# Sliding-window attention inside a stream of projections: one TensorE visit per query tile that holds scores of tile n, transposes of tile n-1 and outputs of tile n-2

## The chip, the cores and the metric

The kernel runs on one core of one Trainium2 chip. The metric is the device time of one execution in microseconds (us), smaller is better; a time given for a kernel is the median of its runs. The engines of the core are called PE (TensorE, matrix products; its weight loads are listed as PEld), DVE (VectorE), ACT (ScalarE), POOL (GpSimd) and SP (SyncE, which here only issues transfers). Each has its own queue of instructions, written in program order.

## What is computed

One inference step of a two-layer decoder trunk with width 2048: 272 prompt rows (16 meta tokens and 256 tokens) and 64 sample rows (8 sequences of 8 tokens). Layer 0 is a gated linear recurrence, layer 1 is sliding-window attention with sinks, 32 query heads of 64 that share 4 key heads, window 128. The change is in layer 1, whose core in the reference is

```python
def sink_attention(q, k, v, mask, sinks):
    s = jnp.einsum('bnqhgd,bnshd->bnhgqs', q, k) * SWA_SCALE
    s = jnp.where(mask[None, :, None, None], s, -jnp.inf)
    sink = sinks.astype(jnp.float32)[None, None, :, :, None, None]
    m = jnp.maximum(jnp.max(s, axis=-1, keepdims=True), sink)
    p = jnp.exp(s - m)
    p = p / (jnp.sum(p, axis=-1, keepdims=True) + jnp.exp(sink - m))
    return jnp.einsum('bnhgqs,bnshd->bnqhgd', p, v)
```

It is used for the prompt (keys of the 144 or 256 positions that a block of queries can see) and for the samples (128 cached keys of each sequence and its own 8 new ones). The result is multiplied with SiLU of a gate projection and goes through the output projection. Everything is float32 to the reader; the large projections are done as three products of float32r halves (weights and inputs are each split into a high and a low part).

## The kernel before

**The stream of projections.** All large products run through one `Stream` (lines 111 to 224). A tile is 128 output columns of a weight; it takes 16 rounds (`kk`), each with three matmuls (L213, L214, L215) on one 128x128 piece of weight, and after each round `step()` is called. A *step* in this document is one such round. `run` also issues, ahead of use, the weight transfers on SP (`raw`, L147, four buffers), the high parts on ACT (`conv_hi`, L158) and the low parts on DVE (`conv`, L169).

**Everything else hangs on steps.** A piece of other work is a Python generator given to `spawn`. `step` (L173) goes through the list in order of spawning and resumes those that are due, at most two per step; `yield k` makes a generator due again k steps later, `yield 0` at the next step. What a generator issues between two yields stands together in the queues of the engines. The order on every engine is thus fixed when the program is written: if PE's next instruction has to wait, the projections behind it wait too.

**Layer 1.** The stream runs the key tiles k0, k1, value tiles v0, v1, then 16 query tiles `q1_j` and 16 gate tiles `g1_j`, then the output projection. When a tile is done, its epilogue spawns a chain. `unfold` (L870) applies the layer norm of layer 0 to the projection: a copy on ACT (L874), two DVE instructions (L876, L878), and an ACT instruction (L880), ten steps in all. Query tile j holds two query heads; four successive tiles share one key head q = j // 4.

**Prompt attention, `prompt_chain(j)` (L1012).** After `unfold`, the query is split (ACT and DVE, L265, L266) and three steps later twelve score matmuls are issued (L1030: keys in 64 rows of the array, the two heads beside each other). One step later DVE scales and masks (L1036), finds maxima (L1039), and `softmax` (L994) goes on: 4 steps later exponentials on ACT (L1003), 3 steps later sums and normalisation on DVE (L1006 to L1009), then 5 steps of pause. Then eight transposes by PE (L1046 to L1050), a step later their copies (ACT L1054, L1055; DVE L1056), 4 steps later the outputs: `vm1` (L1061) and `vm2` (L1064) with 128 key rows, `vm0` (L1067) with 16 key rows, each for the two heads into 64 columns of the array. A step later ACT copies them into `oT` (L1071). Each product that isn't float32r leaves two records.

**Sample attention, `sample_chain(q, u)` (L1073).** It is spawned behind the query tiles j with j % 4 of 1 and 2, so eight times, and handles four sequences: loads of cached keys (`cd`, twice, L1079) and values (`cv`, L1081) on SP, 12 steps later four transposes of keys (L1085) and a copy to `kzs` (L1087), after the fourth query tile of the head 32 small score matmuls (L1097), softmax, four transposes (L1112, L1113), copies (L1116, L1117), and outputs: two products with the 64 new value rows (L1121) and eight with cached values (L1126), copied to `oT` by four DVE instructions (L1131). So the PE part of the attention is made of separate visits between the projections, three for each query tile and four for each sample part.

**PSUM.** The projections use the pool `pj` (three banks), scores `lv` (two), transposes and outputs `mm` (three).

**The end of the attention.** `counted` (L979) keeps the number of unfinished chains in `L["att"]`; the chain of a gate tile (`epi_gg`, L1135) waits with `yield 0` until it is 0, then frees the attention's memory and multiplies gate and output.

## Time and profile before

| | us |
|---|---|
| median of 3 runs | 1181.28 |
| lowest and highest run | 1179.55, 1181.58 |
| the profiled execution | 1182.2 |
| its span, first to last instruction | 1180.4 |

The profile is of one execution. Its page gives busy time for each engine, then the chain of work that ended last, followed back from the last instruction, and groups of instructions by line. Matmuls are pipelined: a matmul is listed with its start and a modelled length of about 0.3 us, while the next can start 0.15 us later, so what one costs is read from the starts. The share of each engine hides that stages differ; by slices of a fortieth of the span (29.5 us), DVE's busy share in tenths and PE's are:

```profile
PE   8999999999999999999999999999999999999995
...
DVE  4766565656565666565668777577878867777674
ACT  4654554544554544554544445566656655554431
```

The attention is issued from about 754 to 952 us, that is, slices 26 to 33.

### The profile page before, as it was taken

What the parts mean: (1) busy time and instruction counts of PE and PEld (TensorE: products, weight loads), DVE (VectorE), ACT (ScalarE), POOL (GpSimd) and SP (SyncE); (2) the same over time, 40 slices, a digit from 0 to 9 for tenths busy, and PEclk for the clock granted to TensorE, in tenths of its full rate; (3) what the DMA queues carried; (4) which work ended last, traced back from release to release, by engine and by line L of the source; (5) the groups of instructions that cost most, each with busy time, mean ns of one, the idle gap of its engine ahead of it and who ended that gap; (6) DMA issues with size and microseconds to landing.
All of it is one profiled execution on the core that took longest, in us unless ns stands there. A gap on an engine that the chain in (4) does not pass through costs nothing.

```text
span 1180.4 us, 26871 instructions
## 1 busy us (share of the span) xinstructions
PE 1159.5 (98%) x10421; PEld 1117.4 (95%) x10421; DVE 789.0 (67%) x2080; ACT 602.8 (51%) x1777; POOL 236.5 (20%) x348
## 2 busy tenths in 40 slices
PE   8999999999999999999999999999999999999995
PEld 8999999999999999999999999988888899999994
DVE  4766565656565666565668777577878867777674
ACT  4654554544554544554544445566656655554431
POOL 3031221211211212211223331000000011154311
PEclk9999999999999999999999999999999999999998
DMA  9654565445555445555455545634244345556532
GB/s 263 181 146 129 162 175 151 136 139 146 162 166 161 131 132 159 161 164 156 119 145 150 142 142 169 184 103 121 87 116 118 93 139 147 150 152 187 140 99 90
DMA packets 328928, 171.51 MB, mean 145 GB/s; under 512 B 19164, under 2 KB 325692, under 8 KB 328758
## 3 DMA queue, kind: packets, MB, share of 16 engines
q1 hardware_dynamic: 327296, 167.77, 50.5%
q8 instruction: 82, 1.34, 0.5%
q10 hardware_dynamic: 960, 1.05, 0.3%
q0 software_dynamic: 544, 0.97, 0.3%
q14 instruction: 46, 0.38, 0.1%
HBM read 156.97 MB, written 14.42 MB: 145 GB/s over the span
## 4 chain that ended last, share of the span: by engine, by line
PE 94%; DMA 2%; POOL 1%; DVE 1%; ACT 1%; issue 0%; SPq 0%; POOLq 0%; DVEq 0%; ACTq 0%
PE pj_q L213 7%; PE pj_g L213 7%; PE pj_g L214 7%; PE pj_g L215 7%; PE pj_q L214 6%; PE pj_q L215 6%; PE pj_f L213 3%; PE pj_i L213 3%; PE pj_i L215 3%; PE pj_i L214 3%; PE pj_f L214 3%; PE pj_f L215 3%; PE pj_z L215 3%; PE pj_z L214 3%; PE pj_z L213 3%; PE pj_y L215 3%
## 5 line engine op out<-in xcount | busy, mean ns | idle before, releaser
L213 PE MATMUL pj_q<-xh,wlo_q 128*128 128x336 f32 (+1 forms) x512 | 167.5, 327 | 0.0
L213 PE MATMUL pj_g<-xh,wlo_g 128*128 128x336 f32 (+1 forms) x512 | 163.4, 319 | 0.0
L214 PE MATMUL pj_q<-xl,whi_q 128*128 128x336 f32 (+1 forms) x512 | 161.0, 314 | 0.0
L215 PE MATMUL pj_q<-xh,whi_q 128*128 128x336 f32 (+1 forms) x512 | 160.8, 314 | 0.0
L214 PE MATMUL pj_g<-xl,whi_g 128*128 128x336 f32 (+1 forms) x512 | 160.7, 314 | 0.0
L215 PE MATMUL pj_g<-xh,whi_g 128*128 128x336 f32 (+1 forms) x512 | 160.4, 313 | 0.0
L213 PEld LDWEIGHTS pj_q<-xh,wlo_q 128*128 128x128 f32 x512 | 96.8, 189 | 5.1 <-issue 2.2
L213 PEld LDWEIGHTS pj_g<-xh,wlo_g 128*128 128x128 f32 x512 | 96.6, 189 | 1.0 <-issue 0.5
L214 PEld LDWEIGHTS pj_q<-xl,whi_q 128*128 128x128 f32 x512 | 97.1, 190 | 0.0
L215 PEld LDWEIGHTS pj_q<-xh,whi_q 128*128 128x128 f32 x512 | 97.0, 190 | 0.0
L214 PEld LDWEIGHTS pj_g<-xl,whi_g 128*128 128x128 f32 x512 | 96.8, 189 | 0.0
L215 PEld LDWEIGHTS pj_g<-xh,whi_g 128*128 128x128 f32 x512 | 96.6, 189 | 0.0
L169 DVE TENSOR_TENSOR wlo_g<-raw_g,whi_g 128x512 fp32r<-128x512 f32 x128 | 90.8, 744 | 0.7 <-ACT whi_g L158 0.6
L169 DVE TENSOR_TENSOR wlo_q<-raw_q,whi_q 128x512 fp32r<-128x512 f32 x128 | 85.0, 684 | 5.4 <-ACT whi_q L158 5.4
L213 PE MATMUL pj_f<-xh,wlo_f 128*128 128x336 f32 x256 | 82.6, 323 | 1.4 <-ACT xh L306 1.4
L213 PE MATMUL pj_i<-xh,wlo_i 128*128 128x336 f32 x256 | 81.6, 319 | 0.0
L213 PE MATMUL pj_z<-oh,wlo_z 128*128 128x336 f32 x256 | 81.3, 318 | 0.0
L214 PE MATMUL pj_f<-xl,whi_f 128*128 128x336 f32 x256 | 81.0, 317 | 0.2 <-DVE xl L308 0.2
L215 PE MATMUL pj_z<-oh,whi_z 128*128 128x336 f32 x256 | 81.1, 317 | 0.0
L214 PE MATMUL pj_i<-xl,whi_i 128*128 128x336 f32 x256 | 81.0, 316 | 0.0
L215 PE MATMUL pj_i<-xh,whi_i 128*128 128x336 f32 x256 | 81.0, 316 | 0.0
L214 PE MATMUL pj_z<-ol,whi_z 128*128 128x336 f32 x256 | 81.0, 316 | 0.0
(405 smaller groups left out, 3193.6 us busy)
## 6 DMA issues: line engine op xcount, KB each, us to landing
raw_z<-in_hgrn_w_out_dram SPq DMA_DIRECT2D x32, 512.0 KB
raw_q<-in_swa_w_in_dram SPq DMA_DIRECT2D x32, 512.0 KB
raw_g<-in_swa_w_in_dram SPq DMA_DIRECT2D x32, 512.0 KB
raw_y<-in_swa_w_out_dram SPq DMA_DIRECT2D x32, 512.0 KB
raw_f<-in_hgrn_w_in_dram SPq DMA_DIRECT2D x30, 512.0 KB
raw_q<-in_hgrn_w_in_dram SPq DMA_DIRECT2D x30, 512.0 KB
raw_i<-in_hgrn_w_in_dram SPq DMA_DIRECT2D x30, 512.0 KB
raw_g<-in_hgrn_w_in_dram SPq DMA_DIRECT2D x30, 512.0 KB
```

Of the source, the lines that this page charges most:

```text
L169: e.nc.vector.tensor_tensor(lo, t.pop(("raw", kc)), hi.bitcast(F32), op=ALU.subtract)
L213: nc.tensor.matmul(ps, lo[:, kk, :], xh, start=first, stop=False)
L214: nc.tensor.matmul(ps, hi[:, kk, :], xl, start=False, stop=False)
L215: nc.tensor.matmul(ps, hi[:, kk, :], xh, start=False, stop=last)
```

## The change

The chains for prompt and samples are replaced by one chain for each query tile, `query_chain(j)`: unfold, split, then 10 steps later `visit(j)`. A visit n issues to PE, without a yield between: the scores of tile n, the eight transposes of tile n-1, four key transposes or three probability transposes of a sample part where `plan` has one, the outputs of tile n-2, and sample outputs where `plan` has them. A step later come the copies out of PSUM and the spawn of the softmax of tile n. Two waiting loops at the head of a visit hold it back until the program has issued the probabilities that it transposes. Behind the last query tile four more visits (16 to 19) follow.

The number of steps in `softmax` is 3 and 3 without a pause at the end. `vm0` has 128 rows, zero from row 16 on, and the tiles `t2` are two fixed ones whose rows from 16 on are zero in the part for `vm0`; `vs` holds the 64 new value rows twice, once in the lower and once in the upper half of the rows, with zeros in the other half, one half for each head. The sample scores lie side by side as 384 columns, so that three transposes take them, and the middle one holds the new keys of both heads. The copy of the 16 rows goes to ACT, sample outputs are copied by one DVE instruction, and the PSUM of key and sample transposes comes from `pj`.

The loads of a sample part are issued in the visit before its key transposes, four steps after it. Its scores are issued 5 steps after the visit with its keys.

The core of the diff; the old chains that it removes stand in the listing above.

```diff
-            for nm, shape in (("vm1", [P, 256]), ("vm2", [P, 256]), ("vm0", [16, 256]), ("vs", [NS, 256]),
+            for nm, shape in (("vm1", [P, 256]), ("vm2", [P, 256]), ("vm0", [P, 256]), ("vs", [P, 2, 256]),
...
+            for q in range(2):
+                L["t2", q] = ap1.tile([P, 512], F32, tag=f"t2_{q}", name=f"t2_{q}")
+            for t in (L["vm0"], L["vs"], L["t2", 0][:, 256:512], L["t2", 1][:, 256:512]):
+                nc.gpsimd.memset(t, 0.0)
...
-                    nc.tensor.transpose(pt[0:64, 384:512], vT[:, 272:336], ident)
+                    v2 = L["ap"].tile([P, P], F32, tag="v2", name=f"v2_{i}", bufs=1)
+                    nc.vector.tensor_copy(v2.rearrange("p (u t) -> p u t", u=2),
+                                          vT[:, 272:336].unsqueeze(1).to_broadcast([P, 2, 64]))
+                    nc.tensor.transpose(pt[:, 384:512], v2, ident)
...
         def epi_qq(j):
             def epi(ps):
-                st.spawn(counted(prompt_chain(j, ps)))
-                if j % 4 in (1, 2):
-                    st.spawn(counted(sample_chain(j // 4, j % 4 - 1)))
+                L["att"] = 1
+                st.spawn(query_chain(j, ps))
             return epi
...
-            yield 4
+            yield 3
             for c, pt in enumerate(parts):
                 nc.scalar.activation(pt, pt, AF.Exp, bias=nmx[:, c:c + 1], accum_out=rsum[:, c:c + 1])
             nc.scalar.activation(sks, sks, AF.Exp)
-            yield 3 if nm is not None else 4
+            yield 3
...
-            yield 5 if nm is not None else 4
...
+            yield 10
+            yield from visit(j, (qh, ql))
+            if j == KT - 1:
+                for n in range(KT, KT + 4):
+                    yield (8, 1, 4, 1)[n - KT]
+                    yield from visit(n)
+                L["att"] = 0
+
+        plan = {}
+        for q in range(4):
+            for u in range(2):
+                n = 4 * q + 3 + u
+                plan.setdefault(n - 1, {})["load"] = q, u
+                plan.setdefault(n, {})["keys"] = q, u
+                plan.setdefault(n + 2 - u * (q == 3), {})["trans"] = q, u
+                plan.setdefault(n + 3 - u * (q == 3), {})["out"] = q, u
+        plan[18]["trans"] = 3, 1
+        plan[17]["trans"] = 3, 0
+        plan[18]["out"] = 3, 0
+        plan.setdefault(19, {})["out"] = 3, 1
+
+        def visit(n, qq=None):
+            ap = L["ap"]
+            todo = plan.get(n, {})
+            while 0 < n <= KT and ("p", n - 1) not in L:
+                yield 0
+            while "trans" in todo and ("sp",) + todo["trans"] not in L:
+                yield 0
+            if n < KT:
+                qh, ql = qq
+                kh, kl = L["kzh", n // 4], L["kzl", n // 4]
+                pa = [lv.tile([P, 512], F32, tag="lv", name=f"s{c}{n}") for c in "ab"]
...
+            j = n - 1
+            if 0 <= j < KT:
+                sm = L["p", j]
+                p1, p2 = pm(f"p1_{j}"), pm(f"p2_{j}")
...
+                    px = e.pj.tile([P, 512], F32, tag="pj", name=f"{'ck' if kind == 'keys' else 'st'}{q}_{u}")
...
+                        for i in range(3):
+                            nc.tensor.transpose(px[:, 128 * i:128 * i + 128],
+                                                L["sp", q, u][:, 128 * i:128 * i + 128], ident)
+            po = None
+            j2 = n - 2
+            if j2 >= 0:
+                po = pm(f"ao{j2}")
+            if 0 <= j2 < KT:
+                vs = slice(64 * (j2 // 4), 64 * (j2 // 4) + 64)
+                t1, t2 = L["t1", j2], L["t2", j2 % 2]
+                for v, t, c0, o, w in (("vm1", t1, 0, 0, 256), ("vm2", t2, 0, 128, 128), ("vm0", t2, 256, 0, 128)):
                     for h in range(2):
+                        nc.tensor.matmul(po[halves2[h], o:o + w], L[v][:, vs], t[:, c0 + w * h:c0 + w * h + w],
+                                         start=v == "vm1", stop=v != "vm1", tile_position=(0, 64 * h),
+                                         skip_group_check=True)
+            if "out" in todo:
...
+                for h in range(2):
+                    nc.tensor.matmul(po[halves2[h], 256:384], L["vs"][:, h, vs], ts[:, 128:256], start=True,
+                                     stop=False, tile_position=(0, 64 * h), skip_group_check=True)
...
             yield 1
+            if n < KT:
+                st.spawn(softmax_chain(n, pa))
+            if 0 <= j < KT:
...
+                nc.scalar.copy(t1, p1)
+                nc.scalar.copy(t2[:, 0:256], p2[:, 0:256])
+                nc.scalar.copy(t2[0:16, 256:512], p2[0:16, 256:512])
+            if "keys" in todo:
+                q, u = todo["keys"]
+                nc.scalar.copy(L["kzs", u].rearrange("p b k -> p (b k)"), px)
+            if 0 <= j2 < KT:
+                nc.scalar.copy(L["oT"][:, j2, 0:256], po[:, 0:256])
+            if "out" in todo:
+                q, u = todo["out"]
+                nc.vector.tensor_copy(
+                    L["oT"][:, 4 * q:4 * q + 4, 256 + 32 * u:288 + 32 * u].rearrange("p j (b t) -> p j b t", t=8),
+                    po[:, 256:384].rearrange("p (b j t) -> p j b t", j=4, t=8))
+            if "trans" in todo:
+                ts = ap.tile([P, 384], F32, tag="ts", name=f"ts{n}", bufs=1)
+                L["ts"] = ts
+                nc.scalar.copy(ts, px[:, 0:384])
+            if "load" in todo:
+                yield 3
...
+            if "keys" in todo:
+                yield 4
+                yield from sample_scores(*todo["keys"])
```

## The prediction

> **What bounds the kernel now.** I read the page first: the share of each engine and the chain that ended last.

> ```profile
> span 1180.4 us, 26871 instructions
> ...
> PE 1159.5 (98%) x10421; PEld 1117.4 (95%) x10421; DVE 789.0 (67%) x2080; ACT 602.8 (51%) x1777; POOL 236.5 (20%) x348
> ...
> PE 94%; DMA 2%; POOL 1%; DVE 1%; ACT 1%; issue 0%; SPq 0%; POOLq 0%; DVEq 0%; ACTq 0%
> ```

> TensorE (PE) holds 94% of the chain: whatever shortens its row of work shortens the kernel. The change touches only the attention, so next comes a window over it, from the first score to the last output.

> ```profile
> 754.00:952.00 198.00, 197.36 (x1814) 173.42 (x1813) 151.60 (x467) 118.31 (x376) 10.92 (x32) 1.00 0.41 113
> ```

> The columns are the length, then busy time of PE, PEld, DVE, ACT and POOL, the clock, DMA share and GB/s. PE idles 0.6 us in 198. By the code 992 of its 1814 matmul records are attention (32 per query tile, 60 per sample part; an fp32 product leaves two). The other 822 are projections. Busy time says little of pipelined matmuls, so I use starts. Here are a score visit and an output visit among projections, from PE's timeline (start, length, instruction).

> ```profile
> 786.34 0.32 PE L215 MATMUL pj_q<-xh,whi_q 128*128 128x322 f32 x1
> ...
> 787.73 0.32 PE L214 MATMUL pj_q<-xl,whi_q 128*128 128x322 f32 x1
> ...
> 788.33 0.31 PE L215 MATMUL pj_q<-xh,whi_q 128*128 128x322 f32 x1
> 788.56 0.65 PE L1061 MATMUL ao<-t,vm 128*64 128x256 f32 x4
> 789.05 0.39 PE L1064 MATMUL ao<-t,vm 128*64 128x128 f32 x4
> 789.36 0.43 PE L1067 MATMUL ao<-t,vm 16*64 16x128 f32 x4
> 789.73 0.41 PE L213 MATMUL pj_q<-xh,wlo_q 128*128 128x322 f32 x1
> 789.98 0.31 PE L214 MATMUL pj_q<-xl,whi_q 128*128 128x322 f32 x1
> ```

> A projection starts every 0.1485 us (20 steps from 792.29 to 795.26, quoted below), 0.15 for short. I price a visit from the start of the last projection before it to the start of the second one behind it, less the two steps of 0.15 that would pass anyway. Scores: 786.34 to 787.73 is 1.39, so **1.09 us**. Outputs: 788.33 to 789.98 is 1.65, so **1.35**. Check: 822 projections at 0.1485 are 122.1; 198 less that leaves 75.9 us for attention.

> **The change part by part.** The other two kinds of visit that matter, transposes of probabilities (with a stretch of bare projections ahead) and sample outputs:

> ```profile
> 792.29 0.31 PE L213 MATMUL pj_q<-xh,wlo_q 128*128 128x322 f32 x1
> ...
> 795.26 0.32 PE L215 MATMUL pj_q<-xh,whi_q 128*128 128x322 f32 x1
> ...
> 796.08 0.27 PE L1049 MATMUL p<-ident,sm 128*128 128x128 f32 x1
> 796.19 0.27 PE L1050 MATMUL p<-ident,sm 128*16 128x128 f32 x1
> ...
> 796.45 0.31 PE L214 MATMUL pj_q<-xl,whi_q 128*128 128x322 f32 x1
> ```

> ```profile
> 804.61 0.30 PE L215 MATMUL pj_q<-xh,whi_q 128*128 128x322 f32 x1
> 804.85 0.43 PE L1121 MATMUL so<-ts,vs 64*64 64x128 f32 x4
> 805.21 0.66 PE L1126 MATMUL so<-ts,cv 128*64 128x32 f32 x16
> ...
> 806.06 0.31 PE L214 MATMUL pj_q<-xl,whi_q 128*128 128x322 f32 x1
> ```

> Eight transposes cost 1.19 less 0.30, **0.89 us**: 0.11 each and nothing for coming and going. So gathering *transposes* saves almost nothing by itself. Sample outputs cost 1.45 less 0.30, **1.15 us**. The price of a visit sits at changes of tile shape (full 128x128, 64 rows, 64 columns): into the outputs 788.33 to 788.56 is 0.23 where 0.15 is the step, and behind them 0.25 to the second projection.

> Two places of before already join visits by chance, which prices the joins:

> ```profile
> 764.27 0.30 PE L215 MATMUL pj_q<-xh,whi_q 128*128 128x322 f32 x1
> ...
> 765.39 0.66 PE L1085 MATMUL ck<-ident,cd 128*128 128x128 f32 x4
> ...
> 766.03 0.31 PE L214 MATMUL pj_q<-xl,whi_q 128*128 128x322 f32 x1
> ```

> ```profile
> 859.05 0.31 PE L215 MATMUL pj_q<-xh,whi_q 128*128 128x322 f32 x1
> ...
> 861.31 0.30 PE L214 MATMUL pj_q<-xl,whi_q 128*128 128x322 f32 x1
> ```

> The first is scores, then four transposes: 1.46 net, where apart they are 1.09 plus 0.44, so 0.07 saved. The second is eight transposes, then scores: 2.26 less 0.30 is 1.96, apart 1.98, so nothing saved.

> The sum on PE:
> 1. Fifteen visits join scores and transposes (n = 1 to 15): 0.07 each is 1.0; before had such a join four times by chance (at 764, 775, 823 and 918 us of PE's timeline), so **0.7 us**.
> 2. Fifteen joins of transposes to outputs: not shown; bounds are the two joins above, 0 to 0.07. I take **0**, the row that leaves full-size transposes for a smaller tile.
> 3. The vm0 product uses 128 zero-padded rows instead of 16, so the outputs keep one tile shape. Now its two passes take 0.37 (789.36 to 789.73) and 0.31 pass before it for two vm2 passes. Passes of 128 columns without a shape change follow at 0.11 (0.21 for two), and leaving costs about 0.09 more, so 0.21 plus 0.31 instead of 0.68: 0.16 saved (bounds 0, if the rows are not the reason, to 0.25 if padding also hides the exit). Sixteen times, **2.5 us**.
> 4. Three sample transposes instead of four: 0.11 by eight, **0.9 us**.
> 5. Sample outputs behind the outputs of a query tile, in the same shape: 2 passes of 0.11 and 8 of 0.06 (the L1126 row: 0.66, of which its last pass some 0.2, over seven steps) are 0.70 instead of 1.15, by six: 2.7. The last two (visits 18 and 19) stand alone and lose only their own row change, 0.1 each. Together **2.9 us**.
> 6. Sample scores and key transposes keep their number and duration: 0.

> That is 7.0 us. Stalls of before go too:

> ```profile
> 760.90 0.31 PE L215 MATMUL pj_q<-xh,whi_q 128*128 128x322 f32 x1
> 761.71 0.33 PE L1046 MATMUL p<-ident,sm 128*128 128x128 f32 x1 [0.51 <-DVE sm L1009]
> ...
> 763.23 0.30 PE L214 MATMUL pj_q<-xl,whi_q 128*128 128x322 f32 x1
> ```

> This transpose visit took 2.33 instead of 1.19, waiting for the softmax: 1.1. The next two show 0.2 more than usual each, two sample visits 0.1 each: **1.8 us**, gone if the new order gives softmax more time. PE's gain is 8.8 us.

> **What is late next.** Each visit n now waits for the normalised probabilities of n-1. The chain of DVE and ACT behind the scores of one tile in before:

> ```profile
> 861.15 0.57 DVE L1036 SCALAR_TENSOR_TENSOR sm<-sa,cst 128x400 f32<-128x400 f32 x1
> ...
> 866.34 1.03 DVE L1009 TENSOR_SCALAR sm<-sm,stat 128x144 f32<-128x144 f32 x4
> ```

> ```profile
> 863.80 0.42 ACT L1003 ACTIVATE sm<-sm,stat 128x144 f32<-128x144 f32 x1 [0.47 <-DVE stat L999]
> ...
> 865.59 0.19 ACT L1004 ACTIVATE stat<-stat 128x4 f32<-128x4 f32 x1
> 866.20 0.36 ACT L1071 COPY oT<-ao 128x256 f32<-128x256 f32 x1
> 866.46 0.56 ACT L880 ACTIVATE qf<-un_q,gb_q 128x320 f32<-128x320 f32 x1
> 866.93 0.61 ACT L158 CAST whi_q<-raw_q 128x512 fp32r<-128x512 f32 x1
> 867.44 0.41 ACT L265 CAST qh<-qf 128x256 fp32r<-128x256 f32 x1
> ```

> It takes 6.2 us: 2.65 to the exponentials, 1.8 for them, 1.8 to the end. After the change, time from scores to the next transposes is the rest of the visit (0.9 transposes, 1.1 outputs: 2.0), 16 steps of three projections (7.2) and the next scores (0.9): 10.1 us. But ACT's copies of the visit, the last only after its outputs, are issued ahead of the exponentials, then qf and a weight cast: 2.0 + 0.15 + 0.36 + 0.56 + 0.61 = 3.7 instead of 2.65. DVE next waits for qh (0.41) behind the exponentials and does ql (0.4) and a weight part (0.7) before the normalisation: the chain ends near 8.5, 1.6 to spare. With key work in the visit about 10.7 of 11.2; with sample outputs, whose copy holds DVE until the visit's end, 10.8 of 11.1; with both (n = 7, 11, 15) 12.7 of 11.9, so PE waits 0.8. That is 2.4 us in three visits, and up to about 1 behind them; DVE instructions overlap by some hundredths each, which gives part back. I take **1.8 us**, bounds 0 and 6.

> [...]

> The rest is cheap. The doubled sample values (one DVE copy ahead of a PE transpose, twice) fall where DVE idles; if not, 0.7 each, a weight part's length. Zeroing four tiles on POOL falls in a stage with POOL at 10.92 of 198. Cache loads on SP:

> ```profile
> 759.01 2.25 SPq L1079 DMA_DIRECT2D cd<-in_cache_swa_k_dram  x2
> ```

> Used by PE at 765.39, so within 6.4 us of issue. New: issued four steps after visit n-1, used 12 steps (5.4) and 2.0 into visit n: 7.4. SP's queue may hold them back behind a weight load by about the difference. I cost it at 0, at worst 1 us by eight loads. PSUM buffers are copied out within a step or two.

> **Sum.** 8.8 less 1.8 is **7.0 us**. The profiled execution took 1182.2 (span 1180.4 and 1.8 around it): 1175.2 in its place. The median of the runs is 1181.28, 0.9 lower: **1174.3**.

> **Rivals.**

> ```profile
> L1071 ACT COPY oT<-ao 128x256 f32<-128x256 f32 x16 | 6.0, 372 | 26.4 <-PE ao L1067 26.4
> ```

> - *Softmax becomes the bound and eats the gain.* For: ACT already idles 26.4 us in front of the output copies, and in the new order these stand ahead of the exponentials. Against: 1.6 us to spare in plain visits. With 0.9 us of waiting behind each of the ten visits that hold key work or sample outputs: 9, so 1181.5. Chance 0.15.
> - *Slower.* The same queue order, but late in every visit: if ACT's and DVE's chain runs over by more than 0.6 us on average in the 15 visits that hold scores and transposes, the gain is gone, beyond 0.75 the kernel is measurably slower. At 1.0 each: 1181.3 - 8.8 + 15 = 1187.5. It decides at a chain of 10.9 us in a plain visit, 2.4 above my 8.5. Chance 0.09.
> - *No new wait at all*: 1181.3 - 8.8 = 1172.5. Chance 0.2.
> - *It does not do what it says*: if the guard on the probabilities shifts a visit by steps, visits stay whole and cost the same; no separate price.

> **How the numbers follow.** Forecast 0.56, no wait 0.2, rival one 0.15, slower 0.09. About 0.2% (2.4 us) is what a measurement can tell. Faster is 0.56 and 0.2: 0.76; same 0.15; slower 0.09. The range reaches from 1171.0 (8.8 and the better end of point 3, 1.4 more) to 1180.0, which takes in waits of up to 7.5 us and so the lower part of the first rival.

> **What would show it.** Right: output visits without the 16-row passes, about 28 attention visits instead of 80, and attention's share near 67 to 70 us instead of 75.9. Wrong: PE rows of p transposes with a wait on DVE sm in most visits, or on a cd load; or vm0 passes still 0.16 and more apart.

## The result and the profile after

| | before | after |
|---|---|---|
| median of the runs, us | 1180.41 (1179.47 to 1181.58, 4 runs) | 1173.17 (1172.38 to 1173.72, 4 runs) |
| ratio, 95% interval | | 0.9937 (0.9925 to 0.995) |
| profiled execution and its span, us | 1182.2, 1180.4 | 1173.12, 1171.3 |

The kernel became 7.2 us faster; 7.0 were forecast. In time the forecast was 1174.3, worked out from a median of 1181.28; taken from the 1180.41 of these four runs, the same 7.0 give 1173.4, and the rival without new waits (8.8) gives 1171.6. As they were put, 1174.3 and 1172.5, the two lie on either side of 1173.17, so between them the waits in the trace decide and not the time. The page of the kernel after, the same three lines as before:

```profile
span 1171.3 us, 26834 instructions
...
PE 1151.3 (98%) x10413; PEld 1116.8 (95%) x10413; DVE 780.1 (67%) x2042; ACT 605.6 (52%) x1787; POOL 234.4 (20%) x352
...
PE 92%; DMA 3%; DVE 2%; ACT 1%; POOL 1%; issue 1%; SPq 0%; POOLq 0%; DVEq 0%
```

TensorE still sets the time. The two spans differ by 9.1 us, more than the medians, and not all of that is the change. The first projection of layer 1, in the timeline of TensorE (start, length, instruction), first before, then after:

```profile
707.03 0.32 PE L213 MATMUL pj_k<-xh,wlo_k 128*128 128x338 f32 x1
```

```profile
705.22 0.32 PE L213 MATMUL pj_k<-xh,wlo_k 128*128 128x338 f32 x1
```

Up to here nothing was changed, and the executions already differ by 1.8 us. So I compare kernels by their medians and, inside one profile, by the attention alone: the sum of its visits, each priced by the prediction's rule (from the last projection before it to the second behind it, less two steps, 0.297). That sum was 76.4 us in 75 visits and is 70.0 in 28. A window over the attention of after says the same:

```profile
754.00:948.00 194.00, 192.78 (x1823) 176.34 (x1822) 144.33 (x429) 122.92 (x387) 8.49 (x33) 1.00 0.42 118
```

984 of the 1823 records are attention (8 fewer than before, one transpose in each sample part); 839 projections at 0.1485 are 124.6, which leaves 69.4 where before left 75.9. TensorE idles 1.2 us.

One joined visit, n = 6, in the timeline of TensorE (only the first record of the scores and of the eight transposes is shown):

```profile
816.90 0.31 PE L215 MATMUL pj_q<-xh,whi_q 128*128 128x322 f32 x1
817.14 0.33 PE L1062 MATMUL sa<-kzh,ql 64*128 64x144 f32 x1
...
818.02 0.33 PE L1069 MATMUL p<-ident,sm 128*128 128x128 f32 x1
...
818.95 0.49 PE L1086 MATMUL st<-ident,sms 128*128 128x128 f32 x3
819.37 1.09 PE L1097 MATMUL ao<-t,vm 128*64 128x256 f32 x12
820.29 0.39 PE L1105 MATMUL ao<-ts,vs 128*64 128x128 f32 x4
820.51 0.61 PE L1110 MATMUL ao<-ts,cv 128*64 128x32 f32 x16
821.05 0.42 PE L213 MATMUL pj_q<-xh,wlo_q 128*128 128x322 f32 x1
821.31 0.30 PE L214 MATMUL pj_q<-xl,whi_q 128*128 128x322 f32 x1
```

From 816.90 to 821.31 less 0.30 is 4.11 us. The six passes of the outputs take 0.92 (819.37 to 820.29), where before took 1.17 (788.56 to 789.73); the sample outputs begin right behind them. Of the 70.0 us, 67.6 is such work and 2.4 is waiting. Where TensorE waits: first the view of its waits from 740 to 960 us (total, times, longest), then its timeline at visit n = 8, with what ended the idle time in brackets:

```profile
PE sa L1062 <- DVE sms L1183: 0.9, 2, 0.5
```

```profile
840.13 0.31 PE L215 MATMUL pj_q<-xh,whi_q 128*128 128x322 f32 x1
840.91 0.30 PE L1062 MATMUL sa<-kzh,ql 64*128 64x144 f32 x1 [0.47 <-DVE sms L1183]
841.24 0.30 PE L1062 MATMUL sb<-kzh,ql 64*128 64x144 f32 x1
```

DVE's timeline beside it:

```profile
839.41 1.02 DVE L1009 TENSOR_SCALAR sm<-sm,stat 128x144 f32<-128x144 f32 x4
840.35 0.42 DVE L1183 SCALAR_TENSOR_TENSOR sms<-ssa,cst 128x128 f32<-128x128 f32 x2
840.68 0.41 DVE L1183 SCALAR_TENSOR_TENSOR sms<-ssb,cst 128x128 f32<-128x128 f32 x2
```

The visit's scores wait, not its transposes. They need the two score banks of PSUM (the pool `lv`), which still hold the sample scores of visit 7; DVE masks these out of the banks at 840.35 and 840.68, behind a normalisation, and `sa` and `sb` start right after. Visits 8 and 12 lose 0.83 us each in this way by the starts (4.39 against 3.56 for visit 4, which does the same work); the view counts only what is left behind the modelled ends, 0.5 each. Another 0.77 us lies at visits 1 and 2, at the transposes.

### The profile page after: what moved, and what is told of

Its sections match the earlier page's. It is cut to its first block, busy times and chain, and to the rows that moved or that the text cites. A ratio compares the mean times of both kernels' runs of the same rounds, so it can differ in the third digit from the quotient of the medians.

```text
span 1171.3 us, 26834 instructions
## 1 busy us (share of the span) xinstructions
PE 1151.3 (98%) x10413; PEld 1116.8 (95%) x10413; DVE 780.1 (67%) x2042; ACT 605.6 (52%) x1787; POOL 234.4 (20%) x352
## 4 chain that ended last, share of the span: by engine, by line
PE 92%; DMA 3%; DVE 2%; ACT 1%; POOL 1%; issue 1%; SPq 0%; POOLq 0%; DVEq 0%
PE pj_g L213 7%; PE pj_g L214 7%; PE pj_g L215 7%; PE pj_q L213 6%; PE pj_q L214 5%; PE pj_q L215 5%; PE pj_f L213 3%; PE pj_i L213 3%; PE pj_f L214 3%; PE pj_i L215 3%; PE pj_f L215 3%; PE pj_i L214 3%; PE pj_y L215 3%; PE pj_y L213 3%; PE pj_y L214 3%; PE pj_z L215 3%
## 5 line engine op out<-in xcount | busy, mean ns | idle before, releaser
L213 PE MATMUL pj_q<-xh,wlo_q 128*128 128x336 f32 (+1 forms) x512 | 163.1, 319 | 0.0
L213 PE MATMUL pj_g<-xh,wlo_g 128*128 128x336 f32 (+1 forms) x512 | 163.0, 318 | 0.0
L214 PE MATMUL pj_g<-xl,whi_g 128*128 128x336 f32 (+1 forms) x512 | 160.6, 314 | 0.0
L214 PE MATMUL pj_q<-xl,whi_q 128*128 128x336 f32 (+1 forms) x512 | 160.5, 314 | 0.0
L215 PE MATMUL pj_g<-xh,whi_g 128*128 128x336 f32 (+1 forms) x512 | 160.3, 313 | 0.0
L215 PE MATMUL pj_q<-xh,whi_q 128*128 128x336 f32 (+1 forms) x512 | 160.3, 313 | 0.0
L213 PEld LDWEIGHTS pj_q<-xh,wlo_q 128*128 128x128 f32 x512 | 96.6, 189 | 2.5 <-issue 1.4
L213 PEld LDWEIGHTS pj_g<-xh,wlo_g 128*128 128x128 f32 x512 | 96.6, 189 | 0.7 <-issue 0.3
L214 PEld LDWEIGHTS pj_g<-xl,whi_g 128*128 128x128 f32 x512 | 96.8, 189 | 0.0
L214 PEld LDWEIGHTS pj_q<-xl,whi_q 128*128 128x128 f32 x512 | 96.7, 189 | 0.0
L215 PEld LDWEIGHTS pj_q<-xh,whi_q 128*128 128x128 f32 x512 | 96.6, 189 | 0.0
L215 PEld LDWEIGHTS pj_g<-xh,whi_g 128*128 128x128 f32 x512 | 96.6, 189 | 0.0
L213 PE MATMUL pj_f<-xh,wlo_f 128*128 128x336 f32 x256 | 82.7, 323 | 0.6 <-ACT xh L306 0.6
L213 PE MATMUL pj_i<-xh,wlo_i 128*128 128x336 f32 x256 | 81.5, 318 | 0.0
L214 PE MATMUL pj_f<-xl,whi_f 128*128 128x336 f32 x256 | 81.2, 317 | 0.2 <-DVE xl L308 0.2
L213 PE MATMUL pj_z<-oh,wlo_z 128*128 128x336 f32 x256 | 81.3, 317 | 0.0
L215 PE MATMUL pj_z<-oh,whi_z 128*128 128x336 f32 x256 | 81.1, 317 | 0.0
L214 PE MATMUL pj_z<-ol,whi_z 128*128 128x336 f32 x256 | 81.0, 316 | 0.0
L215 PE MATMUL pj_f<-xh,whi_f 128*128 128x336 f32 x256 | 80.9, 316 | 0.0
L214 PE MATMUL pj_i<-xl,whi_i 128*128 128x336 f32 x256 | 80.8, 316 | 0.0
```

Source lines behind the costliest of these rows:

```text
L213: nc.tensor.matmul(ps, lo[:, kk, :], xh, start=first, stop=False)
L214: nc.tensor.matmul(ps, hi[:, kk, :], xl, start=False, stop=False)
L215: nc.tensor.matmul(ps, hi[:, kk, :], xh, start=False, stop=last)
```

## The experiments

The kernels ran in three groups beside the result's own, each with its runs of the kernel before (medians 1180.75, 1180.94 and 1181.11), so the ratio is the fair column. "Visits" is the sum described above, from one profile each. For each kernel made from after, the gain over its group's own before differs from after's 7.2 us by what the visits differ, within 0.8 us.

| kernel | median, us | ratio to before, 95% interval | visits, us |
|---|---|---|---|
| after | 1173.17 | 0.9937 (0.9925 to 0.995) | 70.0 |
| before, with `vm0` padded | 1178.82 | 0.9982 (0.9973 to 0.999) | 74.2 |
| after, visits cut in three | 1173.01 | 0.9934 (0.992 to 0.9947) | 69.4 |
| after, sample outputs apart | 1176.01 | 0.9959 (0.9945 to 0.9972) | 71.7 |
| after, `vm0` of 16 rows | 1177.32 | 0.997 (0.9959 to 0.9981) | 72.9 |
| after, sample scores earlier | 1173.14 | 0.9935 (0.9922 to 0.9949) | 69.2 |
| the same, visit 16 later | 1171.99 | 0.9926 (0.9914 to 0.9939) | 68.1 |
| after, 12 steps ahead | 1171.91 | 0.9926 (0.9914 to 0.9939) | 68.0 |
| the last two together | 1171.02 | 0.9912 (0.9897 to 0.9927) | 67.6 |
| after, 6 steps ahead | 1174.9 | 0.9944 (0.9928 to 0.9961) | 70.4 |
| after, 3 steps ahead | 1197.66 | 1.0139 (1.0124 to 1.0155) | 94.4 |

**Where the gain on TensorE comes from.** First the padding alone, in the kernel before.

```diff
-            for nm, shape in (("vm1", [P, 256]), ("vm2", [P, 256]), ("vm0", [16, 256]), ("vs", [NS, 256]),
+            for nm, shape in (("vm1", [P, 256]), ("vm2", [P, 256]), ("vm0", [P, 256]), ("vs", [NS, 256]),
...
+            for q in range(2):
+                L["t2", q] = ap1.tile([P, 512], F32, tag=f"t2_{q}", name=f"t2_{q}")
+            for t in (L["vm0"], L["t2", 0][:, 256:512], L["t2", 1][:, 256:512]):
+                nc.gpsimd.memset(t, 0.0)
...
-            t2 = ap.tile([P, 512], F32, tag="t2", name=f"t2_{j}")
+            t2 = L["t2", j % 2]
...
-                                 t2[0:16, 256 + 128 * h:384 + 128 * h],
+                                 t2[:, 256 + 128 * h:384 + 128 * h],
```

> The kernel before with one part of the change alone: the vm0 product and its probabilities have 128 rows, zero from row 16 on. Theory (changes of tile shape cost, not rows): an output visit, 1.35 us from the last projection before it to the second behind it less 0.30, becomes 1.20; sixteen times that is 2.5 us, so about 1177.9 against 1180.4. Rival (the 16-row product costs no more than a padded one, the gain is all in the joining of visits): unchanged, 1.35 us and 1180.4.

An output visit of it, in TensorE's timeline:

```profile
786.58 0.65 PE L1065 MATMUL ao<-t,vm 128*64 128x256 f32 x4
787.06 0.39 PE L1068 MATMUL ao<-t,vm 128*64 128x128 f32 x4
787.28 0.39 PE L1071 MATMUL ao<-t,vm 128*64 128x128 f32 x4
787.60 0.41 PE L213 MATMUL pj_q<-xh,wlo_q 128*128 128x322 f32 x1
```

The padded product now follows `vm2` after 0.22 instead of 0.31, and its own two passes take 0.32 to the next projection instead of 0.37. The visit fell from 1.35 to 1.21 us, 0.14 for each of 16, so 2.3 us; the visits' sum fell by 2.2 and the median by 1.9. Then the reverse, the product over 16 rows in the kernel after:

```diff
+                    rows = 16 if v == "vm0" else 128
...
-                        nc.tensor.matmul(po[halves2[h], o:o + w], L[v][:, vs], t[:, c0 + w * h:c0 + w * h + w],
+                        nc.tensor.matmul(po[halves2[h], o:o + w], L[v][:rows, vs],
+                                         t[:rows, c0 + w * h:c0 + w * h + w],
```

> The kernel after with the vm0 product over 16 rows again, everything else as after. Theory (a change of tile rows inside a visit has the same price wherever the visit stands): the output part grows by 0.14 to 0.16 us in each of 16 visits, 2.2 to 2.6 us, less where the visit waits anyway: 1175.5 us. [...]

The outputs of its visit 7, which also holds sample outputs:

```profile
832.79 1.24 PE L1098 MATMUL ao<-t,vm 128*64 128x256 f32 x12
833.95 0.44 PE L1107 MATMUL ao<-ts,vs 128*64 128x128 f32 x4
834.22 0.61 PE L1112 MATMUL ao<-ts,cv 128*64 128x32 f32 x16
834.76 0.42 PE L213 MATMUL pj_q<-xh,wlo_q 128*128 128x322 f32 x1
```

The six passes take 1.16 us again and the next product is slower too (0.27 instead of 0.22 to its successor): way in and way back are both paid. Visits without sample outputs grew by 0.145, the six with them by 0.30: 10 by 0.145 and 6 by 0.30 are 3.3. Visit 1 lost its wait of 0.37, so the sum of the visits grew by 2.9. The median grew by 4.2 (3.5 when each kernel is taken against its own runs of before), more than visits explain; the rest isn't explained here, and the two intervals allow it. So the theory held, with a price above its range where full-height products stand behind the small one.

Next, joining as such: scores, transposes and outputs of a visit in three pieces, a step apart.

```diff
                                             stop=i == 2, tile_position=(64 * h, 0), skip_group_check=True)
+                yield 1
+                st.spawn(softmax_chain(n, pa))
             j = n - 1
...
+            if n < KT:
+                yield 1
             po = None
...
             yield 1
-            if n < KT:
-                st.spawn(softmax_chain(n, pa))
```

> The changed kernel with every visit up to 15 cut in three by one step of projections: scores, then transposes, then outputs; sample outputs stay with the outputs, the rest of the order is kept. Theory (only changes of tile shape cost, and transposes have the shape of the projections): 15 joins of scores and transposes lost at 0.07 us and nothing for transposes and outputs, so about 1 us slower, 1174.2. Rival (each visit has a price of its own, some 0.3 us, whatever it holds): 29 visits more, about 8.7 us slower, 1182, all of the gain lost.

With 57 visits instead of 28 the sum is 69.4, below after's 70.0. A cut visit without a wait (scores 1.08, transposes with keys 1.32, outputs 1.21) costs 3.61 where the joined one costs 3.56: 0.05 for two more pieces, some 0.7 us over the whole attention. The cut gives more than that back in waits, because softmax starts right behind the scores and not at the visit's end: visits 1 and 2 wait for next to nothing, and 0.33 us is left at each of 4, 8 and 12. So the time stayed where 1 us more was expected, and the rival, a price on every visit, fell.

Last, sample outputs in a visit of their own, one step later, six times.

```diff
+            if "out" in todo and j2 < KT:
+                yield 1
             if "out" in todo:
```

> The changed kernel with the sample outputs of the six visits that hold them beside outputs of a query tile taken one step later, in a visit of their own. Theory: such a visit costs 1.0 us as visit 19 does, where joined it adds 0.68; six times 0.32 is 1.9 us slower, 1175.1. Rival (the sample outputs gained from their 128 rows and the one shape, not from standing behind other outputs): within 0.5 us of the changed kernel.

Such a visit in TensorE's timeline:

```profile
822.47 0.30 PE L215 MATMUL pj_q<-xh,whi_q 128*128 128x322 f32 x1
822.70 0.44 PE L1107 MATMUL ao<-ts,vs 128*64 128x128 f32 x4
822.97 0.61 PE L1112 MATMUL ao<-ts,cv 128*64 128x32 f32 x16
823.50 0.42 PE L213 MATMUL pj_q<-xh,wlo_q 128*128 128x322 f32 x1
823.76 0.32 PE L214 MATMUL pj_q<-xl,whi_q 128*128 128x322 f32 x1
```

It takes 1.29 less 0.30, 0.99 us, where joined the same products add 0.66 (visits 6 and 5 of after: 4.11 and 3.45). Six times 0.33 is 2.0; the visits' sum grew by 1.7, since the waits at 8 and 12 shrank by 0.17 each. The median grew by 2.8 (2.5 against its own runs of before). The theory held for the visits; what makes up the last 0.8 us isn't shown.

**Where the waits are.** The theory: the banks of the sample scores hold up visits 8 and 12, because in visits 3, 7, 11 and 15 the steps for loads (3) and keys (4) add up, so that their sample scores come 8 steps behind and not 5.

```diff
-                yield 4
+                yield 1 if "load" in todo else 4
                 yield from sample_scores(*todo["keys"])
```

> The changed kernel with the sample scores of visits 3, 7, 11 and 15 three steps earlier, five steps behind the visit as in the others. Theory (the waits of 0.85 us at the scores of visits 8 and 12 are for the two PSUM banks that the sample scores of visits 7 and 11 still hold, because DVE masks them only behind the normalisation): both waits go, 1.7 us faster, 1171.5, and the mask of visit 7 runs while DVE would wait for qh. Rival (DVE is simply late by that much behind visits with both key work and sample outputs, as the prediction had it): the wait moves to the transposes of visits 8 and 12 with about the same length, time unchanged.

Visits 8 and 12 fell from 4.39 to 3.56, as the theory has it, and the time stayed: 1173.14. The gain is found again at visit 16, from TensorE's timeline:

```profile
932.52 0.63 PE L1082 MATMUL ck<-ident,cd 128*128 128x128 f32 x4 [0.80 <-DMA cd<-in_cache_swa_k_dram]
```

Visit 16 stands a fixed 8 steps behind visit 15's last yield, so it came three steps earlier with the sample scores of visit 15. The load of its keys did not: SP issues it 8.7 us behind the start of visit 15 in both kernels. In after it is issued at 928.89 and used at 933.64, 4.75 us later without a wait; here it is issued at 927.85 and used at 932.52, 4.67 us later and as soon as it has landed. By the starts the visit waits 1.0 us for the load (the view shows 0.8) and 0.3 for probabilities: 3.81 instead of 2.54 us. So the banks were the cause, and removing it only moved the wait. With three steps given back there:

```diff
-                    yield (8, 1, 4, 1)[n - KT]
+                    yield (11, 1, 4, 1)[n - KT]
```

> The changed kernel with the sample scores of visits 3, 7, 11 and 15 three steps earlier, and visit 16 kept where it was (eleven steps behind visit 15's last action instead of eight), so that its cache load and its probabilities are not asked for earlier. Theory: the waits at n = 8 and 12 are gone as in the run with the earlier sample scores alone, and the 1.3 us that visit 16 waited there for its load and probabilities are not paid, so about 1.7 us faster than the changed kernel, 1171.5. Rival (the load is late for a reason of its own): visit 16 still takes over 3 us, 1173.

Visit 16 is back at 2.54, and the gain stays: 1171.99. The other way to the same end is more time, two steps more between split and visit:

```diff
-            yield 10
+            yield 12
             yield from visit(j, (qh, ql))
```

> The changed kernel with a visit twelve steps behind its query's split instead of ten, so that the split of the next query is issued four steps behind the visit, ahead of the exponentials, instead of six, behind them. Theory (DVE's 1.7 us of idling for the high query part, which ACT does behind the exponentials, is what makes the chain from scores to probabilities long): that idling goes, the probabilities are ready about 1 us earlier (0.14 us ahead of the transposes of visits 7, 11 and 15 becomes about 1.2), and the waits at visits 2, 3, 9 and 13 of the order (n = 1, 2, 8, 12; 2.5 us in all) shrink by at least 1.5 us: 1171.5. Rival (ACT's and DVE's amount of work is the limit, not their order): spare time and waits as before, 1173.2.

Visits 1 and 2 lost their waits (1.90 and 3.12 us instead of 2.27 and 3.51), 8 and 12 kept 0.2 each; 1171.91, near the theory's 1171.5. The cause it names shows too: DVE's waits for `qh` between 740 and 960 us fell from 18.1 us to 3.4. Both edits together:

> The kernel after with 12 instead of 10 steps ahead of a visit, sample scores one step after the copies where the visit also issues loads, and 11 steps ahead of visit 16. Theory (all waits on PE in the attention are the probabilities' and the score banks', and both are now late by no visit): as the run with 12 steps alone, less the 0.4 us left at visits 8 and 12, so 1171.5 us, attention stretch near 296, and no row of PE in the attention with a wait behind it. Rival (the two edits do the same thing and each has already taken all there is): 1171.9, no lower than either alone. Rival two (visit 16 waits again for a cache load, since everything is shifted): about 1 us more, 1173.

1171.02 us, the lowest median, though its interval overlaps those of the two edits alone. The view of TensorE's waits has no row between 740 and 960 us, and the visits take 67.6 us, just the work that was left in after when its waits were subtracted. The window over its attention:

```profile
754.00:948.00 194.00, 194.00 (x1838) 178.38 (x1837) 146.68 (x432) 123.81 (x390) 8.78 (x33) 1.00 0.44 120
```

TensorE is busy for the whole 194 us.

**How many steps the split must lead.** In before, scores came three steps behind the split and no visit of scores waited for it. The same three in the kernel after:

```diff
-            yield 10
+            yield 3
             yield from visit(j, (qh, ql))
```

> The changed kernel with a visit three steps behind its query's split, as the scores were in the kernel before, instead of ten. Theory (the gain is in shapes and joins; the distance only sets what ACT and DVE do between scores and probabilities, and the split then falls 13 steps behind the visit before, out of that chain): within 1.5 us of the changed kernel, 1172.5 to 1174.0, with the waits at n = 8 and 12 smaller and at most some tenths of waiting for the low query part. Rival (the distance of ten steps carries the gain, because scores would wait for the split): a wait of 0.3 us or more in front of most score groups, at least 4 us slower, 1177 or more.

1197.66 us: the rival was right, and its price too small. The waits of TensorE, then its timeline at visit 7:

```profile
PE sa L1062 <- DVE ql L266: 17.3, 9, 3.1
```

```profile
827.82 0.32 PE L215 MATMUL pj_q<-xh,whi_q 128*128 128x322 f32 x1
830.33 0.31 PE L1062 MATMUL sa<-kzh,ql 64*128 64x144 f32 x1 [2.19 <-DVE ql L266]
...
831.37 0.27 PE L1070 MATMUL p<-ident,sm 128*128 128x128 f32 x1
831.48 0.38 PE L1069 MATMUL p<-ident,sm 128*128 128x128 f32 x1
831.65 0.42 PE L1070 MATMUL p<-ident,sm 128*128 128x128 f32 x1
831.87 0.42 PE L1072 MATMUL p<-ident,sm 128*128 128x128 f32 x1
```

Why the low half is late stands in DVE's timeline, and what DVE waits for in ACT's:

```profile
821.28 0.29 DVE L1129 COPY oT<-ao 128x128 f32<-128x128 f32 x1 [4.98 <-ACT oT L1126]
...
826.78 0.55 DVE L876 SCALAR_TENSOR_TENSOR un_q<-nmb,gb_q,pj_q 128x320 f32<-128x320 f32 x1 [1.44 <-ACT gb_q L874]
...
829.77 0.41 DVE L266 TENSOR_TENSOR ql<-qf,qh 128x256 fp32r<-128x256 f32 x1
```

```profile
824.72 0.42 ACT L1003 ACTIVATE sm<-sm,stat 128x144 f32<-128x144 f32 x1 [2.56 <-DVE stat L999]
...
826.61 0.14 ACT L874 COPY gb_q<-pj_q 128x2 f32<-128x2 f32 x1
```

DVE's copy of the sample outputs holds its queue until the end of visit 6 (821.28); masks, maxima, then four exponentials on ACT follow, and only behind them stands the small copy of the next query's gamma and beta, `gb_q`. `unfold`, normalisation and split all stand behind that, and the split ends at 830.18. The second part of the loss is the clock; the window right behind the wait:

```profile
831.60:835.00 3.40, 3.40 (x21) 2.54 (x21) 0.00 (x0) 1.80 (x4) 0.00 (x0) 0.51 0.44 132
```

The row gives the length, busy times, and then 0.51 as the granted clock; transposes start 0.21 us apart where 0.11 was usual. Visit 7 takes 8.09 us instead of 4.21: about 2.3 of waiting and 1.6 of half clock. Over all visits, 17.3 us of waits and five stretches of half clock at 1.7 us each are 25.8 of the 26.8 us above the 67.6 of work. To tell the two apart, six steps:

> The kernel after with 6 steps instead of 10 between the split and the visit. It separates the two parts of the loss at 3 steps: the wait for the low half of the query, and the lower granted clock behind it. Theory A (only the lead of the split decides, the clock falls only behind long idle stretches of TensorE): three steps more are 1.35 us, the nine waits of 1.9 us shrink to about 0.6, some 5 us in all; the clock stays at 1.00 in the attention; about 1178 us. Theory B (any wait at that place lowers the clock): the same short waits, but transposes 0.2 us apart behind them and a granted clock under 0.99 in the attention, about 1184 us. If the wait were for something that is not tied to the split's lead, waits of 1.9 us would stay: 1197.

```profile
821.69 0.18 ACT L874 COPY gb_q<-pj_q 128x2 f32<-128x2 f32 x1
...
824.30 0.42 ACT L1003 ACTIVATE sm<-sm,stat 128x144 f32<-128x144 f32 x1 [1.91 <-DVE stat L999]
```

This is ACT's timeline at the same place: `gb_q` now stands ahead of the exponentials. The split, DVE's L266, ends at 828.20 just as the last projection has started (828.02), and only 0.1 us is lost. Over the attention one wait for the split is left (1.1 us at visit 1) beside the two for the score banks (0.6 each), the clock stays at 1.00, and the visits' sum is 70.4, within 0.4 of after. Theory A was right about the clock but priced the waits at 5 us. They don't shrink in proportion to the steps: from DVE's copy (821.28 there, 821.46 here) to the end of the split it takes 8.90 us with three steps and 6.74 with six, and 1.44 of the difference is the wait for `gb_q`. This is read from the two traces; no run moved that copy alone. The median, 1174.9, is 1.7 above after's (1.0 when each is taken against its own runs of before), and the intervals overlap; what lies beyond the 0.4 of the visits isn't settled.

## Why the prediction was right, and where it was not

- **The gain on TensorE** (forecast 7.0 of work and 1.8 of stalls, 8.8 together). Visits fell from 76.4 to 67.6 us without the new waits, 8.8. Its parts:
  - *Points 1 and 2, joins*: 0.7 and 0 forecast; cutting them again cost 0.7.
  - *Point 3, padding*: 2.5 forecast; 2.3 measured alone in before. The reason given was right, a change of tile rows, and the cost lies at the way in (first starts 0.21 apart where 0.11 is usual) and between the product's two passes (0.16). The way out is no dearer where a projection follows (0.21 with either height); where full-height products follow, as in the run with 16 rows in after, it takes 0.20 instead of 0.11.
  - *Point 4, three transposes*: visit 4 (four transposes of keys) takes 3.56 us, visit 5 (three of probabilities) 3.45, so 0.11 for one and 0.9 for eight, as forecast.
  - *Point 5, sample outputs*: a join costs 0.66 where 0.70 was taken, against 1.15 in before, so six give 2.9; of that 2.0 is the joining (the run with sample outputs apart) and the rest the product's own shape. The two that stand alone lost 0.15 each. Together 3.2 where 2.9 was forecast.
  - *Point 6* held: sample scores take 0.69 in both kernels.
- **"It does not do what it says"** is out: 28 visits instead of 75 (of the prediction's 80, five stood joined by chance).
- **The new waits** (1.8 forecast, 2.4 found). The size was nearly right by luck: 0.8 was priced for each wait and 0.83 found, but for another resource. The step that failed reads "PSUM buffers are copied out within a step or two": for the score banks that is false, since the masks that empty them stand in DVE's queue behind a normalisation. In the trace the mask begins at 840.35, 0.08 before the end of the normalisation issued ahead of it, though the last of its scores had started at 836.48. The prediction had counted what stands ahead in DVE's queue for the probabilities and not for the buffers.
- **The chain of the softmax.** From the last score to the last normalised probability it was put at 12.7 us for visits with keys and sample outputs. It is 11.1 for n = 7 (scores end at 829.32, the row L1009 at 840.43). The step that failed is adding the two delays, 2.2 for keys and 2.3 for outputs: with keys alone the chain takes 8.8 to 10.1 us (n = 3, 4, 8 and 12), with outputs alone 11.0, with both 11.1. So the two don't add up; both are a wait for the same end of the visit. For visits with sample outputs alone 10.8 of 11.1 was forecast, and 11.0 of 11.15 is found at n = 10 (scores end 864.11, normalisation 875.12, transposes 875.26): 0.14 us to spare. So the softmax rival was near, but it didn't come about; twelve steps raise the margin to 1.4 us.
- **Visits 1 and 2** weren't among the forecast waits: there the transposes do wait for probabilities (0.77 us together). The step that failed is the time of 10.1 us from scores to the next transposes, taken for every plain visit. Visit 0 holds nothing but scores and visit 1 no outputs, so that there are only 8.1 and 9.0 us (read where neither visit waits, in the run with both edits), while the chain, put at 8.5, takes 8.8 and 10.0 in after.
- **Cache loads at nothing** held in after. They became a wait as soon as visit 16 moved three steps: a load that took 4.67 us had 4.75 in after.
- **The ten steps** between split and visit: the prediction took the lead of the split as given and didn't price it. It is what makes the rest possible; with three, the kernel is slower than before by 1.39%.

In sum, 8.8 less 2.4 is 6.4 us by the visits, against a median that fell by 7.2. The other 0.8 lies outside the attention's visits. In the two profiles, the stretch from the first projection of the output product to the end takes 134.7 us before and 133.9 after, but in the kernels made from after it takes 134.1 to 134.5, so at most a part of it can be the change's, and no run shows by what.

## What to carry to other kernels

Gathering matmuls into one visit is worth little by itself (0.05 us for two cuts here); matmuls of one tile shape put side by side, if need be by padding with zero rows, were worth 0.14 to 0.33 us each time. Where visits become longer, list everything that waits for a visit's end on ACT and DVE, in the order of their queues, buffers included, and check whether the next visit's operands stand behind it: here a lead of three steps instead of ten cost over 24 us. A wait that is removed early in such a chain should be looked for at the next place where steps are counted by hand.

## What the runs showed of the hardware

```profile
804.21:807.62 3.41, 2.17 (x22) 1.80 (x20) 2.88 (x8) 1.90 (x4) 0.36 (x2) 1.00 0.45 131
845.17:848.58 3.41, 1.47 (x17) 1.36 (x18) 3.16 (x11) 1.59 (x6) 0.00 (x0) 1.00 0.27 77
```

```profile
8.97:12.38 3.41, 1.76 (x9) 1.08 (x8) 1.77 (x4) 1.64 (x4) 0.00 (x0) 1.00 1.04 287
12.38:15.79 3.41, 3.41 (x14) 3.35 (x14) 1.07 (x2) 0.79 (x2) 0.00 (x0) 0.50 1.15 270
```

In the traces of before and after, the beats at full clock that half clock followed held 1.76 us of TensorE's work (8.97 to 12.38 us of before) and, at the end of both kernels, 1.38 (1166.09 to 1169.50 of before, 1157.25 to 1160.66 of after). The emptiest that full clock followed, 583.81 to 587.22 us of after, held 1.84. Ends of matmuls are modelled, so these numbers are only as good as they are. In the run with three steps, full clock followed the beat around visit 5 with its 2.17 us and half clock the one with 1.47; around the waits of 1.2 us at visits 5, 9 and 13 the clock stays at 1.00 (in 5.5 us around each TensorE is busy for 4.26). None of these beats was idle as a whole: the one of before with 1.76 us of work was idle for 1.65 of its 3.41, and the clock fell.

Executions of the same code differ before layer 1 begins: its first projection starts at 707.03 us in before, 705.22 in after and 705.17 in the run with both edits, so that a difference of two profiled spans can't be read to better than some 2 us.
